# Half-width units for the sixteen least used experts of a mixture-of-experts stage

## The chip, the cores and the metric

The kernel runs as one program on one core of a Trainium2 chip. The metric is the device time of one execution in microseconds (us). The kernel before took 2224.62 us (median of three runs, 2224.14 to 2226.86).

## The reference, cut to what matters

The reference runs a two-layer network of attention mixers and dense feed-forward blocks over 256 tokens of 1024 features, then a block whose last part is a mixture of 32 experts. Only that last part is touched:

```
logits = jnp.dot(xf, w_router) + b_router
vals, idx = lax.top_k(logits, TOP_K)
gate = jax.nn.softmax(vals, axis=-1)
...
up = jnp.dot(xb, w_up[eb]) + b_up[eb]
glu, lin = jnp.split(up, 2, axis=-1)
glu = jnp.minimum(glu, SWIGLU_LIMIT)
lin = jnp.clip(lin, -SWIGLU_LIMIT, SWIGLU_LIMIT)
act = glu * jax.nn.sigmoid(SWIGLU_ALPHA * glu) * (lin + 1.0)
return jnp.dot(act, w_down[eb]) + b_down[eb]
```

Every token goes to 4 of 32 experts (`TOP_K` is 4), so 1024 token-expert pairs are spread over the 32 experts. Each expert has an up matrix of 1024 x 2048 and a down matrix of 1024 x 1024 in float32: 12 MiB, all of which is read once. With the reference's inputs the pairs fall unevenly. The three experts that the kernel takes first whatever their use (0, 11 and 22) have 5, 44 and 43 pairs. The other 29, from the most to the least used, have 99, 86, 78, 63, then 59, 49, 47, 47, 46, 30, 29, 27, and then 25, 25, 23 and so on down to 3.

## The kernel before, in words

Everything before the experts is as it was, but for one small table of constants and the order of a few instructions around it. The experts' stage starts near 1228 us of the span and lasts to its end.

An expert's weights come from main memory as 12 chunks of 128 x 2048 float32 (1 MiB each): chunks 0 to 3 for the gate half of the up product, 4 to 7 for the linear half, 8 to 11 for the down product. They land in a ring of 22 buffers (`RING`). SyncE's queue issues the loads in the order of first use (lines 1945 and 1948), and each waits until the chunk that had its buffer has been used for the last time. For the first 22 loads the buffer is memory that the mixer before used, so these wait for the mixer's last readers and writers there. A semaphore lane is used by every eighth load, so at most eight are under way.

The work is done in units of 64 slots (`CAP`). The tokens of a unit are gathered by a product with a one-hot matrix (`pick`, `gather`, lines 1730 to 1755), two units at a time. Then `products` (line 1778) multiplies: the 64 gathered tokens are the stationary operand of 128 rows x 64 columns, and a chunk streams past in two halves of 512 columns, the first half into PSUM partitions 0 to 63, the second into 64 to 127, so that the 1024 output columns stand as two column blocks one above the other. `expert_gate` and `expert_act` do the activation on VectorE and ScalarE, `expert_turn` transposes, `expert_down` multiplies again, and `expert_out` (line 1837) adds the result to the four accumulators of the output, by a scatter matrix `sp` that `spread` (lines 1757 to 1773) makes. The result is split into a rounded part `yh` and a rest `yl`.

Four of the experts (the four most used besides the three that are fixed) get two units each; all others get one. That makes 36 units. The down product of a unit is done between the two up products of the next. A pair of units has one gather, in four pieces between the products.

If any expert has more pairs than its units have slots, a flag is set and `overflow` runs further passes over all experts at the end.

Of the kernel before, what the change touches and what calls it, by code (L numbers as in the profile page):

```python
# [19 lines left out]
P = 128  # L20
# [136 lines left out]
DOUBLE = (15, 9, 23, 5)  # L157
STEPS = list(range(len(FIXED))) + list(DOUBLE)
STEPS += [s for s in range(NE) if s not in STEPS]
# [3 lines left out]
NU = len(UNITS)  # L163


def _consts3():
    p = np.arange(P)
    slots = np.broadcast_to(TAKEN + np.arange(4 * CAP, dtype=np.float32), (P, 4 * CAP))
# [7 lines left out]
    single = np.broadcast_to(np.array([s not in DOUBLE for s in range(NE)], np.float32), (P, NE))  # L176
    return np.ascontiguousarray(np.concatenate([slots, iota, sel, stri, rank, block, (p % NE).astype(np.float32)[:, None], key,
                                                single], 1))
# [3 lines left out]
M_IOTA = M_SLOTS + 4 * CAP  # L182
# [6 lines left out]
M_SINGLE = M_KEY + NE  # L189
# [132 lines left out]
class Kernel:  # L322
# [1248 lines left out]
    def moe_consts(self, pool):  # L1571

        nc, v, ins = self.nc, self.nc.vector, self.ins
        self.slots = pool.tile([P, 4 * CAP], F32, name="slots")
# [6 lines left out]
        self.single = pool.tile([P, NE], F32, name="single")  # L1581
# [6 lines left out]
        for dst, src in ((self.wr, ins["w_router"]), (self.brc, ins["b_router"].partition_broadcast(P)),  # L1588
                         (self.slots, ins["consts3"][:, M_SLOTS:M_SLOTS + 4 * CAP]),
# [5 lines left out]
                         (self.single, ins["consts3"][:, M_SINGLE:M_SINGLE + NE]), (self.btab, self.btab_dram)):  # L1595
# [27 lines left out]
    def moe_head(self, mp, first_group):  # L1623
# [8 lines left out]
        self.over = mp.tile([1, 3], I32, name="over")  # L1632
        self.order = mp.tile([1, NE], I32, name="order")
        with ExitStack() as ctx:
# [60 lines left out]
            cnt = tp.tile([1, NE + 3], F32, name="cnt")  # L1695
            v.scalar_tensor_tensor(cnt[:, 3:], qs[0:1, NE:2 * NE], float(CAP), self.single[0:1], ALU.is_gt, ALU.mult)
            v.tensor_reduce(cnt[:, 1:2], cnt[:, 3:], AX.X, ALU.max)
            v.tensor_reduce(cnt[:, 2:3], qs[0:1, NE:2 * NE], AX.X, ALU.max)
            v.tensor_scalar(cnt[:, 2:3], cnt[:, 2:3], 2.0 * CAP, None, ALU.is_gt)
            v.tensor_reduce(cnt[:, 0:1], cnt[:, 1:3], AX.X, ALU.max)  # L1700
            v.tensor_copy(self.over, cnt[:, 0:3])
# [28 lines left out]
    def pick(self, of):  # L1730

        v = self.nc.vector
        pr = self.gp.tile([P, 2, len(of) * CAP], F32, tag="pr", name="pr", bufs=2)
        for t in range(2):
            for i, (pos, r) in enumerate(of):
                v.tensor_scalar(pr[:, t, i * CAP:(i + 1) * CAP], self.slots[:, r * CAP:(r + 1) * CAP], pos[:, t:t + 1],
                                self.r2[t], ALU.is_equal, ALU.mult)
        return pr

    def gather(self, xs, j, pr, ps):  # L1740
# [16 lines left out]
    def spread(self, pos, r, gate, pool, bufs):  # L1757

        nc, v = self.nc, self.nc.vector
        pf = self.gp.tile([P, 2, 2, CAP], F32, tag="pf", name="pf")  # L1760
        slots = self.slots[:, r * CAP:(r + 1) * CAP].unsqueeze(1).to_broadcast([P, 2, CAP])
        ps = self.pv()
        for t in range(2):
            v.tensor_scalar(pf[:, t], slots, pos[:, t:t + 1], None, ALU.is_equal)
            nc.tensor.transpose(ps[:, t * P:(t + 1) * P], pf[:, t].rearrange("p a b -> p (a b)"), self.ident)
        for t in range(2):
            nc.tensor.matmul(ps[:, S:S + 1], pf[:, t].rearrange("p a b -> p (a b)"), gate[:, t:t + 1], start=t == 0,  # L1767
                             stop=t == 1, skip_group_check=True)
        sp = pool.tile([P, S], F32R, tag="sp", name="sp", bufs=bufs)
# [12 lines left out]
    def expert_up(self, part, xg, sel, chunk, between={}):  # L1782

        ps = self.sc()
# [4 lines left out]
        self.last_up = self.products(ps, sel, self.btab[:, part], False, True).ins  # L1789
        return ps  # L1790

    def expert_gate(self, ps, pool, gl, sg):
        v = self.nc.vector
        gl = pool.tile([P, 512], F32, tag=gl, name="gl")
        sg = pool.tile([P, 512], F32, tag=sg, name="sg")
# [5 lines left out]
    def expert_act(self, ps, gl, pool, ln="aT"):  # L1801
        v = self.nc.vector
        ln = pool.tile([P, 512], F32, tag=ln, name="ln")
# [4 lines left out]
    def expert_turn(self, a, pool):  # L1808

        pt = self.pt()  # L1810
        for c in range(4):
            self.nc.tensor.transpose(pt[:, c * P:(c + 1) * P], a[:, c * P:(c + 1) * P], self.ident)  # L1812
        aT = pool.tile([P, 512], F32, tag="aT", name="aT")
        self.nc.scalar.copy(aT, pt)
        return quads(aT)

    def expert_down(self, aT, sel, gs, chunk, pool, yh, yl):
        nc, v = self.nc, self.nc.vector
        ps = self.sc()
        self.products(ps, sel, self.btab[:, 2], True, False)  # L1820
        for c in range(4):
            for h in range(2):
                self.products(ps, aT[:, c, 64 * h:64 * h + 64], chunk(8 + c)[:, h * D:h * D + D],
# [427 lines left out]
```

## Time and profile before

| | |
|---|---|
| median of three runs | 2224.62 us |
| profiled execution | 2222.24 us |
| its span in the profile | 2220.5 us |
| TensorE busy | 2184.6 us (98%) |
| VectorE, ScalarE busy | 1152.8 us (52%), 772.7 us (35%) |
| loads of expert chunks | 384 MiB, in 383 loads of 1 MiB and two of 512 KiB |
| granted TensorE clock, mean | 0.996 of full |

The profile shows one execution. In the page's view of 40 equal slices, a digit is the busy share in tenths; PEclk is the clock that TensorE was granted, in tenths of full speed; DMA is the mean busy share of the 16 DMA engines and GB/s what they moved. A float32 product appears as two records of MATMUL, so "x8" of such a group are four products. PEld is TensorE's load of the stationary operand. "SPq" is SyncE's queue, which issues the loads. The text after "<-" in square brackets names what an engine had waited for.

### The profile page before, as it was taken

Reading aid. Unit: us, or ns where it says so; the run is one execution under the profiler, and the core shown is the slowest. Engines: PE = TensorE matmul, PEld = TensorE weight load, DVE = VectorE, ACT = ScalarE, POOL = GpSimd, SP = SyncE. Lnnn points to the kernel's source line nnn. Section 1 sums busy time; section 2 is a strip of 40 time slices with the busy share of each in tenths; the row PEclk is TensorE's granted clock in tenths of the full one; section 3 lists DMA queues with packets and bytes.
Section 4 is the critical chain, followed back from the end, with each engine's and each line's share of the span. In section 5 each row is a group of like instructions: output and inputs, shape, how many; then the busy total and the mean of one; then the engine's idle time right before and its main releaser. Section 6 shows DMA issues by size and latency. Waiting matters only on the chain.

```text
span 2220.5 us, 36133 instructions
## 1 busy us (share of the span) xinstructions
PE 2184.6 (98%) x14352; PEld 1516.0 (68%) x14352; DVE 1152.8 (52%) x2537; ACT 772.7 (35%) x1431; POOL 95.2 (4%) x147
## 2 busy tenths in 40 slices
PE   8999999999999999999999999999999999999997
PEld 8999889999999989999987433333333333333332
DVE  6777778776889887875886322222222222222122
ACT  5545556454444555544574211111111111111111
POOL 1001001221001001001000000000000000000000
PEclk9999999999999999999999999999999999999998
DMA  6655326776664534765534999998999999999995
GB/s 245 209 183 183 133 105 225 270 270 231 247 245 165 190 105 162 256 246 172 186 143 200 420 421 397 374 421 341 379 421 374 387 421 421 421 384 421 421 421 205
DMA packets 93536, 634.10 MB, mean 286 GB/s; under 512 B 12960, under 2 KB 14112, under 8 KB 18224
## 3 DMA queue, kind: packets, MB, share of 16 engines
q1 hardware_dynamic: 87072, 619.63, 71.5%
q0 software_dynamic: 2288, 7.28, 0.9%
q10 hardware_dynamic: 4000, 4.81, 0.7%
q8 instruction: 115, 1.88, 0.3%
q14 instruction: 61, 0.50, 0.1%
HBM read 626.16 MB, written 5.51 MB: 284 GB/s over the span
## 4 chain that ended last, share of the span: by engine, by line
PE 92%; DVE 5%; DMA 1%; issue 1%; ACT 1%; SPq 0%; ACTq 0%; DVEq 0%
PE sc L1778 35%; PE acc L349 11%; PE acc L351 11%; PE acc L350 11%; PE sc L349 3%; PE sc L350 3%; PE sc L351 3%; PE acc L1837 2%; PE pv L1746 2%; PE pt L1746 2%; PE sc L789 1%; DVE wlo L309 1%; PE pv L867 1%; PE pt L1812 1%; DVE xg L1755 1%; PE pt L854 1%
## 5 line engine op out<-in xcount | busy, mean ns | idle before, releaser
L1778 PE MATMUL sc<-ring,xg 128*64 128x512 f32 x2304 | 554.3, 601 | 0.0
L349 PE MATMUL acc<-xh,whi 128*128 128x256 f32 (+1 forms) x1776 | 507.7, 286 | 7.0 <-ACT whi L308 7.0
L351 PE MATMUL acc<-xh,wlo 128*128 128x256 f32 (+1 forms) x1776 | 505.1, 284 | 1.1 <-DVE wlo L309 1.1
L350 PE MATMUL acc<-xl,whi 128*128 128x256 f32 (+1 forms) x1776 | 501.8, 283 | 1.8 <-DVE xl L399 1.8
L309 DVE TENSOR_TENSOR wlo<-wraw,whi 128x1024 fp32r<-128x1024 f32 (+1 forms) x362 | 440.8, 1220 | 115.7 <-ACT whi L308 112.7
L308 ACT CAST whi<-wraw 128x1024 fp32r<-128x1024 f32 (+1 forms) x362 | 375.5, 1043 | 311.3 <-issue 101.3
L349 PEld LDWEIGHTS acc<-xh,whi 128*128 128x128 f32 x1776 | 338.0, 190 | 9.9 <-ACT whi L308 7.2
L350 PEld LDWEIGHTS acc<-xl,whi 128*128 128x128 f32 x1776 | 338.3, 190 | 2.7 <-DVE xl L399 2.6
L351 PEld LDWEIGHTS acc<-xh,wlo 128*128 128x128 f32 x1776 | 337.9, 190 | 1.6 <-DVE wlo L309 1.6
L1778 PEld LDWEIGHTS sc<-ring,xg 128*64 128x64 f32 x2304 | 146.9, 136 | 241.5 <-issue 226.7
L1778 PE MATMUL sc<-ring,aT 128*64 128x512 f32 x1152 | 253.6, 592 | 0.0
L349 PE MATMUL sc<-hh,whi 128*128 128x256 f32 x704 | 199.7, 284 | 0.0
L350 PE MATMUL sc<-hl,whi 128*128 128x256 f32 x704 | 199.2, 283 | 0.0
L351 PE MATMUL sc<-hh,wlo 128*128 128x256 f32 x704 | 199.2, 283 | 0.0
L1778 PEld LDWEIGHTS sc<-ring,aT 128*64 128x64 f32 x1152 | 82.6, 137 | 149.9 <-issue 141.5
L1755 DVE TENSOR_SCALAR xg<-pv,acol,modc 128x64 f32<-128x64 f32 x140 | 38.4, 336 | 245.2 <-PE pv L1746 245.2
L349 PEld LDWEIGHTS sc<-hh,whi 128*128 128x128 f32 x704 | 135.0, 192 | 2.5 <-issue 2.5
L350 PEld LDWEIGHTS sc<-hl,whi 128*128 128x128 f32 x704 | 135.1, 192 | 0.0
L351 PEld LDWEIGHTS sc<-hh,wlo 128*128 128x128 f32 x704 | 135.1, 192 | 0.0
L1828 DVE SCALAR_TENSOR_TENSOR yl<-sc,gs,yh 128x512 fp32r<-128x512 f32 x36 | 27.0, 751 | 206.5 <-ACT yh L1827 206.5
L1771 ACT CAST sp<-pv 128x256 fp32r<-128x256 f32 x36 | 13.4, 372 | 257.1 <-PE pv L1767 257.1
L1827 ACT ACTIVATE yh<-sc,gs 128x512 fp32r<-128x512 f32 x36 | 24.7, 687 | 212.0 <-PE sc L1778 212.0
(497 smaller groups left out, 2437.5 us busy)
## 6 DMA issues: line engine op xcount, KB each, us to landing
ring<-in_experts_dram SPq DMA_DIRECT2D x383, 1024.0 KB, 19.7
wraw<-in_weights_dram SPq DMA_DIRECT2D x178, 1024.0 KB, 4.9
wraw<-in_w_ada_dram SPq DMA_DIRECT2D x24, 1024.0 KB, 5.0
skew<-g POOLq DMA_DIRECT2D x8, 264.0 KB, 6.1
wraw<-in_weights_dram SPq DMA_DIRECT2D x4, 512.0 KB, 3.5
bias_dram<-b POOLq DMA_DIRECT2D x8, 208.0 KB, 5.3
w<-skew POOLq DMA_DIRECT2D x8, 200.0 KB, 5.8
bias<-bias_dram ACTq DMA_DIRECT2D x1, 1040.0 KB, 10.2
```

Source lines behind the costliest of these rows:

```text
L308: self.nc.scalar.copy(hi[:, a:b], r[:, o + a:o + b])
L309: self.nc.vector.tensor_tensor(lo[:, a:b], r[:, o + a:o + b], hi[:, a:b], ALU.subtract)
L349: nc.tensor.matmul(out, wh, xh, start=first, stop=False, skip_group_check=True)
L350: nc.tensor.matmul(out, wh, xl, start=False, stop=False, skip_group_check=True)
L351: nc.tensor.matmul(out, wl, xh, start=False, stop=last, skip_group_check=True)
L789: nc.tensor.matmul(ps[:, t * S:(t + 1) * S], q[:, t * P:(t + 1) * P], k, start=t == 0, stop=t == 1, skip_group_check=True)
L1746: nc.tensor.matmul(ps[:, i * w:(i + 1) * w], self.x[:, j + i, t * P:(t + 1) * P], pr[:, t], start=t == 0 and i == 0, stop=t == 1, skip_gro ...
L1755: nc.vector.tensor_scalar(x[:, j + i], o, a, b, ALU.mult, ALU.add)
L1778: m = self.nc.tensor.matmul(ps[64 * h:64 * h + 64], lhs, rhs[:, h * 512:h * 512 + 512], start=first, stop=last, skip_group_check=True)
L1827: nc.scalar.activation(yh, ps, AF.Copy, scale=gs)
L1828: v.scalar_tensor_tensor(yl, ps, gs, yh, ALU.mult, ALU.subtract)
L1837: self.nc.tensor.matmul(self.out[t][h], sp[rows, t * P:(t + 1) * P], ys[q][rows], start=False, stop=q == 1, skip_group_check=True)
```

## The change

The experts are sorted into kinds by their place in the order of use (`KINDS`): three fixed ones (F) and nine of middle use (M) with one unit of 64 slots, the four most used (D) with two of 64, and the sixteen least used (L) with one unit of 32 slots. There are 36 units as before. The order in which the experts come is now a pattern of seven, four times over: M L D L M L L.

For an L unit `products` issues four products of 32 columns by 256 in place of two of 64 by 512: the 1024 output columns stand as four column blocks in PSUM partitions 0 to 31, 32 to 63, 64 to 95 and 96 to 127. Everything after it in that unit works on 256 columns instead of 512. `spread` makes two copies of the scatter matrix for an L unit, each with the rows of the other column block set to zero, and `expert_out` issues eight products of 256 columns in place of four of 512 for each half of the tokens, each with 64 rows as before. A gather serves up to 128 slots, so up to four units; there are 15 gathers instead of 18. The evacuation of a gather is one instruction for all its units instead of one for each. The overflow path and the test that leads to it are rewritten for the new number of slots. The table `slots` becomes 128 columns instead of 256, and a table `part` of two columns is added; both lie below the ring in the same stack of memory, so that the ring's buffers move by 504 bytes in each partition.

```diff
 FIXED = (0, 11, 22)
-DOUBLE = (15, 9, 23, 5)
...
+KINDS = "FFFM" + 4 * "MLDLMLL"
+STEPS = [s for kind in "FDML" for s in range(NE) if KINDS[s] == kind]
 RANK = [STEPS.index(s) for s in range(NE)]
-UNITS = [(s, r) for s in range(NE) for r in range(1 + (s in DOUBLE))]
+UNITS = [(s, o, n) for s in range(NE)
+         for o, n in {"D": ((0, CAP), (CAP, CAP)), "L": ((0, CAP // 2),)}.get(KINDS[s], ((0, CAP),))]
...
-        self.slots = pool.tile([P, 4 * CAP], F32, name="slots")
+        self.slots = pool.tile([P, 2 * CAP], F32, name="slots")
...
+        self.part = pool.tile([P, 2], F32, name="part")
...
-    def gather(self, xs, j, pr, ps):
+    def gather(self, x, j, pr, ps):
...
-            for n, x in enumerate(xs):
-                o = ps[:, i * w + n * CAP:i * w + n * CAP + CAP]
-                if j % 4 == 0 or j == 6 and len(xs) == 1:
-                    nc.scalar.activation(x[:, j + i], o, AF.Identity, bias=b, scale=a)
-                else:
-                    nc.vector.tensor_scalar(x[:, j + i], o, a, b, ALU.mult, ALU.add)
...
+            o = ps[:, i * w:(i + 1) * w]
+            if j % 4 == 0:
+                nc.scalar.activation(x[:, j + i], o, AF.Identity, bias=b, scale=a)
+            else:
+                nc.vector.tensor_scalar(x[:, j + i], o, a, b, ALU.mult, ALU.add)
...
-        nc.scalar.copy(sp, ps[:, 0:S])
+        k = CAP // n
+        sp = pool.tile([P, 2, S], F32R, tag="sp", name="sp", bufs=bufs)[:, 0:k]
+        for c in range(k):
+            nc.scalar.activation(sp[:, c], ps[:, 0:S], AF.Copy, scale=1.0 if k == 1 else self.part[:, c:c + 1])
...
     def products(self, ps, lhs, rhs, first, last):
-        for h in range(2):
-            m = self.nc.tensor.matmul(ps[64 * h:64 * h + 64], lhs, rhs[:, h * 512:h * 512 + 512], start=first, stop=last,
+        n = lhs.shape[1]
+        w = D * n // P
+        for h in range(P // n):
+            m = self.nc.tensor.matmul(ps[n * h:n * h + n, 0:w], lhs, rhs[:, h * w:h * w + w], start=first, stop=last,
                                       skip_group_check=True)
...
     def expert_out(self, ys, sp, ts=(0, 1)):
+        w = ys[0].shape[1]
         for t in ts:
             for q in range(2):
-                for h in range(2):
-                    rows = slice(64 * h, 64 * h + 64)
-                    self.nc.tensor.matmul(self.out[t][h], sp[rows, t * P:(t + 1) * P], ys[q][rows], start=False, stop=q == 1,
-                                          skip_group_check=True)
+                for c in range(sp.shape[1]):
+                    for h in range(2):
+                        rows = slice(CAP * h, CAP * h + CAP)
+                        self.nc.tensor.matmul(self.out[t][h][:, c * w:c * w + w], sp[rows, c, t * P:(t + 1) * P], ys[q][rows],
+                                              start=False, stop=q == 1, skip_group_check=True)
```

Two places show how instructions moved. The first is TensorE's order in one unit, from the down product of the unit before on: `aT` is the transposed activation, `xg` the gathered tokens, `yh` and `yl` the two parts of a result, and the last figure is partitions x columns of the output. Before, for a unit of 64 slots after a unit of 64:

```order
L1778 MATMUL sc<-ring,aT 64x512 x16
L1778 MATMUL sc<-ring,xg 64x512 x6
L1837 MATMUL acc<-yh,sp 128x512 x2
L1837 MATMUL acc<-yl,sp 128x512 x2
L1778 MATMUL sc<-ring,xg 64x512 x4
```

And now, for an L unit after an L unit:

```order
L1794 MATMUL sc<-ring,aT 32x256 x32
L1794 MATMUL sc<-ring,xg 32x256 x12
L1858 MATMUL acc<-yh,sp 128x256 x4
L1858 MATMUL acc<-yl,sp 128x256 x4
L1794 MATMUL sc<-ring,xg 32x256 x8
```

The products of such a unit are twice as many, each of half the columns out of half the stationary operand; their places in the unit are the same.

The second place is SyncE's queue at the first loads into the ring, with the semaphores that each waits for: PE, DVE and Pool count the instructions of TensorE, VectorE and GpSimd, DMAHW and DMASW with a number are the lanes of loads. Before:

```order
L1948 DMA ring<-in_experts_dram 128x2048 [waits PE_49,Pool_49]
L1948 DMA ring<-in_experts_dram 128x2048
L1948 DMA ring<-in_experts_dram 128x2048 [waits DMAHW4_49,DVE_49]
L1948 DMA ring<-in_experts_dram 128x2048 [waits DMASW4_49,DMASW3_49,DMASW6_49,DMASW2_49,DMASW0_49]
L1948 DMA ring<-in_experts_dram 128x2048 [waits DMAHW1_49,PE_49]
L1948 DMA ring<-in_experts_dram 128x2048 [waits DMAHW3_49,DMAHW2_49]
L1948 DMA ring<-in_experts_dram 128x2048 x2
```

And now:

```order
L1973 DMA ring<-in_experts_dram 128x2048 [waits PE_49,Pool_49]
L1973 DMA ring<-in_experts_dram 128x2048 x2
L1973 DMA ring<-in_experts_dram 128x2048 [waits DMASW4_49,DMASW3_49,DMASW6_49,DMASW2_49,DMASW0_49]
L1973 DMA ring<-in_experts_dram 128x2048 [waits DMAHW2_49]
L1973 DMA ring<-in_experts_dram 128x2048 [waits DMAHW3_49,DVE_49]
L1973 DMA ring<-in_experts_dram 128x2048 [waits DMAHW5_49,DMAHW4_49,DVE_49]
L1973 DMA ring<-in_experts_dram 128x2048
```

Before, the third load waits for VectorE: by the count it waits for, for the mixer's last weight split (line 309), which VectorE began at 1192.11 us in that trace. Now the seventh load waits for that count, and the sixth for that of an earlier weight split, the one that VectorE began at 1159.98 us in the trace of the kernel before. The counts that the new first load waits for are of transposes at line 1429 of the kernel before, which ran before 1098 us. The waits for DMASW lanes are for transfers of GpSimd's queue that are long past in both.

## Rows read from the trace of the kernel before

**Rows 1.** The page: the span, and the part in 40 equal slices of 55.5 us each.

```profile
span 2220.5 us, 36133 instructions
...
PE   8999999999999999999999999999999999999997
...
PEclk9999999999999999999999999999999999999998
DMA  6655326776664534765534999998999999999995
GB/s 245 209 183 183 133 105 225 270 270 231 247 245 165 190 105 162 256 246 172 186 143 200 420 421 397 374 421 341 379 421 374 387 421 421 421 384 421 421 421 205
```

**Rows 2.** Busy time of the engines in stretches: the stretch, its length, then busy us and instructions of PE, PEld, DVE, ACT and POOL, the granted clock, the DMA engines' busy share and GB/s.

```profile
1161.00:1194.00 33.00, 32.67 (x195) 23.08 (x194) 25.26 (x134) 20.65 (x67) 0.00 (x0) 1.00 0.00 1
1230.00:1370.00 140.00, 139.45 (x704) 54.23 (x704) 33.29 (x92) 18.39 (x42) 0.00 (x0) 1.00 1.01 421
1370.00:1400.00 30.00, 29.72 (x150) 11.23 (x148) 6.31 (x17) 3.56 (x8) 0.00 (x0) 1.00 0.87 348
1550.00:1580.00 30.00, 30.00 (x150) 10.84 (x146) 4.24 (x9) 4.15 (x9) 0.00 (x0) 1.00 0.80 323
1194.00:2190.00 996.00, 990.99 (x5016) 392.39 (x5018) 229.59 (x639) 139.97 (x321) 0.00 (x0) 1.00 0.98 403
```

**Rows 3.** The waits, of TensorE from 1194 to 2206 us and of SyncE's queue from 1150 us on: who waited for whom, us in total, times, the longest.

```profile
PE pv L1765 <- DVE xg L1755: 4.7, 17, 0.3
...
SPq L1945 <- PE sc L1778: 244.0, 108, 22.1
...
SPq L1948 <- DVE md L1328: 39.2, 1, 39.2
```

**Rows 4.** The chain of work that ended last, two of its pieces: start us, us, what. They are the same place in a pair of units, sixteen pairs apart.

```profile
1281.30 13.46 PE sc L1778 x64
...
2149.21 13.46 PE sc L1778 x64
```

**Rows 5.** The timeline of TensorE within one pair of units: start us, us, engine, line, operation, output and operands, shapes, records.

```profile
1339.39 7.04 PE L1778 MATMUL sc<-ring,aT 128*64 128x512 f32 x32
1346.26 2.75 PE L1778 MATMUL sc<-ring,xg 128*64 128x512 f32 x12
...
1375.05 1.16 PE L1746 MATMUL pt<-pr,x 128*128 128x128 f32 x8
1376.14 1.08 PE L1778 MATMUL sc<-ring,xg 128*64 128x512 f32 x4
1377.15 0.50 PE L1837 MATMUL acc<-yh,sp 64*128 64x512 f32 x2
```

**Rows 6.** The timeline around line 507, much earlier in the kernel, the one place where four products of 32 columns stand side by side: TensorE, and its loads of the stationary operand.

```profile
480.73 1.06 PE L507 MATMUL pt<-mod,ones 128*32 128x512 f32 x8
481.72 0.38 PE L349 MATMUL sc<-hh,whi 128*128 128x256 f32 x1
...
480.73 0.16 PEld L507 LDWEIGHTS pt<-mod,ones 128*32 128x32 f32 x8
```

**Rows 7.** The loads of expert chunks: the timeline of SyncE's queue at the first of them, the page's row of their issues (KB each and median us from issue to landing), and two weight splits in the timeline of VectorE.

```profile
1151.03 0.86 SPq L1948 DMA_DIRECT2D ring<-in_experts_dram  x2
1193.35 59.23 SPq L1948 DMA_DIRECT2D ring<-in_experts_dram  x30
...
ring<-in_experts_dram SPq DMA_DIRECT2D x383, 1024.0 KB, 19.7
...
1159.98 1.23 DVE L309 TENSOR_TENSOR wlo<-wraw,whi 128x1024 fp32r<-128x1024 f32 x1 [1.65 <-ACT whi L308]
...
1192.11 1.21 DVE L309 TENSOR_TENSOR wlo<-wraw,whi 128x1024 fp32r<-128x1024 f32 x1
```

**Rows 8.** Busy time in stretches of 2 us, where the stream of chunks sets in and where it ends; columns as in rows 2.

```profile
1194.00:1196.00 2.00, 2.00 (x12) 0.92 (x12) 1.75 (x6) 0.76 (x2) 0.00 (x0) 1.00 0.83 201
...
2188.00:2190.00 2.00, 2.00 (x12) 0.98 (x14) 0.00 (x0) 0.00 (x0) 0.00 (x0) 1.00 0.71 287
```

**Rows 9.** Busy time at the start of the kernel, the one stretch in which TensorE waits often; columns as in rows 2.

```profile
5.00:10.00 5.00, 3.73 (x16) 3.30 (x16) 4.08 (x8) 4.92 (x13) 1.61 (x2) 1.00 1.01 371
10.00:15.00 5.00, 2.87 (x14) 2.46 (x15) 2.70 (x5) 3.48 (x8) 3.91 (x4) 0.79 1.00 423
15.00:20.00 5.00, 5.00 (x26) 5.00 (x26) 2.81 (x4) 3.92 (x5) 0.00 (x0) 0.53 0.99 374
20.00:25.00 5.00, 5.00 (x44) 5.00 (x43) 4.79 (x13) 1.46 (x2) 0.00 (x0) 1.00 0.60 197
```

**Rows 10.** The timeline of all engines at the end: the last down product, the two parts of its result, and the last product into the accumulators.

```profile
2196.18 7.09 PE L1778 MATMUL sc<-ring,aT 128*64 128x512 f32 x32
...
2203.31 0.69 ACT L1827 ACTIVATE yh<-sc,gs 128x512 fp32r<-128x512 f32 x1 [8.16 <-PE sc L1778]
...
2204.03 0.75 DVE L1828 SCALAR_TENSOR_TENSOR yl<-sc,gs,yh 128x512 fp32r<-128x512 f32 x1 [8.58 <-ACT yh L1827]
...
2204.84 0.73 PE L1837 MATMUL acc<-yl,sp 64*128 64x512 f32 x4
```

More of the change, by code (lines that the diff above doesn't have):

```diff
@@ L175, in _consts3 @@
     block = (p[:, None] // NE == p[None, :] // NE).astype(np.float32)
-    single = np.broadcast_to(np.array([s not in DOUBLE for s in range(NE)], np.float32), (P, NE))
+    room = np.broadcast_to(np.array([sum(n for x, _, n in UNITS if x == s) for s in range(NE)], np.float32), (P, NE))
+    part = np.stack([p // 32 % 2 == c for c in range(2)], 1).astype(np.float32)
     return np.ascontiguousarray(np.concatenate([slots, iota, sel, stri, rank, block, (p % NE).astype(np.float32)[:, None], key,
-                                                single], 1))
+                                                room, part], 1))
 M_SLOTS = 0
-M_IOTA = M_SLOTS + 4 * CAP
+M_IOTA = M_SLOTS + 2 * CAP
 M_SEL = M_IOTA + NE
@@ L188 @@
 M_KEY = M_COL + 1
-M_SINGLE = M_KEY + NE
+M_ROOM = M_KEY + NE
+M_PART = M_ROOM + NE
 def _expert_chunks(up, down):
@@ L1788, in expert_up @@
                 f()
-        self.last_up = self.products(ps, sel, self.btab[:, part], False, True).ins
+        self.last_up = self.products(ps, sel[:, 0:n], self.btab[:, part], False, True).ins
         return ps
@@ L1808, in expert_turn @@
     def expert_turn(self, a, pool):
+        w = a.shape[1]
         pt = self.pt()
-        for c in range(4):
+        for c in range(w // P):
             self.nc.tensor.transpose(pt[:, c * P:(c + 1) * P], a[:, c * P:(c + 1) * P], self.ident)
         aT = pool.tile([P, 512], F32, tag="aT", name="aT")
-        self.nc.scalar.copy(aT, pt)
-        return quads(aT)
+        self.nc.scalar.copy(aT[:, 0:w], pt[:, 0:w])
+        n = w // P
+        m = P * w // D
+        return [aT[:, k % n * P + k // n * m:k % n * P + k // n * m + m] for k in range(KD)]
     def expert_down(self, aT, sel, gs, chunk, pool, yh, yl):
         nc, v = self.nc, self.nc.vector
-        ps = self.sc()
-        self.products(ps, sel, self.btab[:, 2], True, False)
+        n = aT[0].shape[1]
+        w = D * n // P
+        ps = self.sc()[:, 0:w]
+        self.products(ps, sel[:, 0:n], self.btab[:, 2], True, False)
         for c in range(4):
             for h in range(2):
-                self.products(ps, aT[:, c, 64 * h:64 * h + 64], chunk(8 + c)[:, h * D:h * D + D],
-                              False, c == 3 and h == 1)
-        yh = pool.tile([P, 512], F32R, tag=yh, name="yh")
-        yl = pool.tile([P, 512], F32R, tag=yl, name="yl")
+                self.products(ps, aT[4 * h + c], chunk(8 + c)[:, h * D:h * D + D], False, c == 3 and h == 1)
+        yh, yl = [pool.tile([P, 512], F32R, tag=t, name=t)[:, 0:w] for t in (yh, yl)]
         nc.scalar.activation(yh, ps, AF.Copy, scale=gs)
@@ L1886, in more_slots @@
                 sel = self.select(bsel, ep)
-                for r in rs:
+                for r in range(2):
                     raw = {}
@@ L1963, in moe, with group @@
         groups, spreads = {}, {}
-        def group(u, pos):
-            of = UNITS[u:u + 2]
-            pr = self.pick([(pos(e), r) for e, r in of])
-            xs = [gp.tile([P, KD, CAP], F32, tag="xg", name="xg", bufs=3) for _ in of]
-            groups.update({u + i: x for i, x in enumerate(xs)})
-            return [lambda j=j, ps=(self.pt, self.pv)[j // 2 % 2]: self.gather(xs, j, pr, ps()) for j in range(0, KD, 2)]
+        def group(first, pos):
+            of = UNITS[slice(*first)]
+            pr = self.pick([(pos(e), o, n) for e, o, n in of])
+            x = gp.tile([P, KD, P], F32, tag="xg", name="xg", bufs=2)[:, :, 0:pr.shape[2]]
+            at = 0
+            for i, (_, _, n) in enumerate(of):
+                groups[first[0] + i] = x[:, :, at:at + n]
+                at += n
+            return [lambda j=j, ps=(self.pt, self.pv)[j // 2 % 2]: self.gather(x, j, pr, ps()) for j in range(0, KD, 2)]
         def first_group():
-            for f, ps in zip(group(0, lambda e: self.pos[:, :, FIXED[e]]), (self.sc, self.sc, self.pt, self.pv)):
+            for f, ps in zip(group(GROUPS[0], lambda e: self.pos[:, :, FIXED[e]]), (self.sc, self.sc, self.pt, self.pv)):
                 f(ps=ps)
@@ L2011, in down @@
                 return self.expert_down(o["a"], o["sel"], o["gs"], o["chunk"], ep, "yh", "yl")
+        starts = {first: (first, end) for first, end in GROUPS}
         old = None
-        for u, (e, r) in enumerate(UNITS):
+        for u, (e, _, _) in enumerate(UNITS):
             n = {}
@@ L2023, in moe @@
             steps = post() if last else [lambda: slots(u + 1)]
-            if u % 2 and not last:
-                steps = group(u + 1, lambda e: self.spos[:, :, e]) + steps
+            if u + 1 in starts:
+                steps = group(starts[u + 1], lambda e: self.spos[:, :, e]) + steps
             if u:
```

102 lines of the change are left out of this document (55 added, 47 removed).

## The prediction

> **What bounds the kernel now.** I read the 40 slices of the page first [rows 1]. The reader should see two halves: up to slice 21 the DMA engines are busy half of the time, and from slice 23 on they stand at 9 with 421 GB/s, with single slices at 341 to 397. TensorE is at 9 everywhere and its clock full. So in the experts' stage two resources are near their end at once, and the question is which of them waits for the other.
>
> Next the waits [rows 3]. TensorE waits for nothing but 4.7 us of gather evacuations; it never waits for a chunk. SyncE's queue waits 244 us for TensorE's products, up to 22.1 us at a time: it has a chunk to load and no free buffer. So TensorE sets the pace and the transfers follow. The stretches [rows 2] show how close it is: 1.01 busy share and 421 GB/s from 1230 to 1370 us, but 0.87 from 1370 to 1400 and 0.80 from 1550 to 1580.
>
> The slack of the transfers is counted so. A chunk is 1,048,576 bytes, at 421 GB/s 2.49 us; that fits the 19.7 us from issue to landing with eight under way [rows 7]. Two chunks are loaded early, at 1151 us, the other 382 in one stream that sets in at 1194.4 us (0.83 of 2 us at once) and ends at 2189.4 us (0.71 of 2 us) [rows 7, 8]. 382 x 2.49 = 951 us, so without a stop it would end at 2145.6 us: 43.8 us of the stream are stops. The mean of 403 GB/s over 996 us [rows 2] says the same, 4.3% or 43 us.
>
> TensorE's pace: the same place in a pair of units comes 16 pairs later at 2149.21 instead of 1281.30 us [rows 4], 54.24 us for a pair and 27.12 for a unit; 36 units take 976 us. An expert's 12 chunks take 29.9 us, 32 experts 956. A single unit is faster than its transfer, a double one (54.2) far slower; together TensorE is slower by 20 us.
>
> **The change part by part.** *Products of the L units.* Sixteen products of a down part take 6.87 us (1339.39 to 1346.26) [rows 5], 0.86 us for a pair of column blocks; the three parts of a unit 20.6 us, and 6.5 us are gather, transposes, scatter and the rest. For an L unit the same weights stream as four blocks of 256 columns. From below that is half, 0.43 us for the four, if four blocks run side by side as two do; from above 0.86 us, if they run two by two. The nearest rows: four products of 32 columns by 512 take 1.06 us with the next instruction 0.99 us after their start [rows 6]; two of 64 by 512 take 1.08 and 1.01 us (1376.14 to 1377.15) [rows 5]. Four blocks cost what two cost, so I take half. Their eight loads of the stationary operand took 0.16 us [rows 6], less than 0.43. An L unit is then 27.12 - 10.3 = 16.8 us, 16 of them save 165 us. The activation, the transposes and the two parts of the result on half the columns only get shorter, off the path except at the end. Three gathers fewer save 3 x 4 pieces x 1.1 us (1375.05 to 1376.14) [rows 5] = 13 us. The second copy of the scatter matrix is one more ScalarE instruction per L unit; ScalarE is busy 140 of 996 us [rows 2], which hides it. TensorE's demand falls from 976 to 20 x 27.12 + 16 x 16.8 - 13 = 798 us.
>
> *The first loads.* The ring lies 504 bytes elsewhere, and so the queue's wait of 39.2 us [rows 3] stands before the seventh load, no longer before the third. Loads three to five can go at 1151 us, the sixth when the weight split begun at 1159.98 us is done; the seventh goes at 1193.35 us, as the third did [rows 7]. From 1161 to 1194 us the DMA engines are idle, 0.00 and 1 GB/s [rows 2], so four chunks land in time that nothing uses: 378 instead of 382 are left. That is 4 x 2.49 = 10 us, which counts only if the transfers set the end. The bounds are 0 us, if one of the other waits is late, and 10; I take 10.
>
> *What is late next.* With 798 us of work against 941 us of transfers TensorE waits and the chunks set the pace: the gain on TensorE beyond the stops of the stream is lost. The stream ends at 1194.4 + 378 x 2.49 = 2135.6 us plus what stops remain. A stop needs a full ring. TensorE's first product is near 1228 us in both, when some 20 chunks have landed; it gains on the transfers by 2.8 us with each full unit and 13.1 us with each L unit, and gives back 24 us at a double expert, four times. One pattern of seven (two M, four L, one D) takes TensorE 175.7 us and the transfers 209, so after the first pattern TensorE is always close behind the stream. Only the first double expert finds a well filled ring. From below the stops are 0, from above the 43.8 us of now; the nearest is one stop like that of 1370 to 1400 us, 0.13 x 30 = 4 us [rows 2]. I take 4: the stream ends at 2139.6 us.
>
> *The end.* Now the last product ends at 2203.3 and the span at 2220.5 us, 17.2 us later [rows 1, 10]. The last half chunk is used some 2 us after it lands (a landing like the ones above, then two rounds of products). The two parts of the result, 0.69 and 0.75 us [rows 10], halve: -0.7 us. Against that, I add 0.7 us for a clock that may stand low there (below). 2139.6 + 2 + 17.2 = 2158.8 us.
>
> *Sum.* Span 2158.8 against 2220.5, -61.7 us. The profiled execution was 1.7 us above its span (2222.24), so 2160.5; the median of the runs is 2.4 us above the profiled execution, so 2163 us for the median.
>
> **The clock.** TensorE will be idle for 15% of the stage, in L stretches for 44%. At the kernel's start there is such a stretch [rows 9]: with 2.87 of 5 us busy, waiting for operands, the granted clock fell to 0.79 and then to 0.53, close to the lower level of 1.2 GHz, and after 5 us of full work it was 1.00 again. So I expect dips in the L stretches. At the lower level an L unit takes 33.6 us, more than its 29.9 us of chunks; TensorE falls behind, is then busy without a gap, and gets the clock back, as the last of these rows shows. The lag is a few us, and the ring takes it.
>
> The Trainium skill, in "TensorE: Matmul & The Clock Gate", section "HAM oscillation — how this bites in real kernels", says that a kernel whose work on each loaded slice is shorter than the wait for the next starts every slice at the low clock. By that rule every chunk of an L unit would be worked at 1.2 GHz; it is the rival below, and the first three of rows 9 agree with the fall.
>
> The skill's "DMA: Bandwidth & Descriptors", section "Where 436 GB/s comes from", has main memory bind one core at about 358 GB/s. By that 378 chunks would take 1107 us and the stream would end at 2302 us. The trace disagrees: 421 GB/s for 140 us [rows 2].
>
> **The rivals.**
> *Low clock all along (slower).* If the clock stayed low through all L units, they would take 16 x 33.6 = 538 us, with the others 1080 us against 976: 2222 + 104 = 2326 us. It decides from the point where an L unit costs what a unit costs now, 27.1 us, 1.6 times its time at full clock; up to 24.9 us ((941 - 542) / 16) the transfers still hide it. For it speaks the fall in rows 9; against it the recovery there, since a unit too slow for its chunks leaves no gaps.
> *Column blocks two by two.* Then an L unit keeps its 20.6 us of products, and only the gathers' 13 us and some shorter steps go: 2224 - 17 = 2207 us. Against it speaks line 507 [rows 6].
> *Stops remain.* The double experts keep filling the ring, or slow L units pile up before them, and half of the 43.8 us stays: 2163 + 18 = 2181 us. For it: the stops of now [rows 2]; against it: the balance of a pattern, 176 against 209 us.
> *The overflow pass runs.* It would load every expert again, at least 956 us more. With the reference's inputs the sixteen least used hold at most 25 pairs for 32 slots, the next nine 59 for 64, the doubles 99 for 128, so I give it nothing.
>
> **How the numbers follow.** The transfers set the pace: 0.78, with 2154 to 2175 us as its own range (no stop at one end, no early loads at the other). Stops remain: 0.10. Two by two: 0.05. Low clock all along: 0.04. Something else of no effect: 0.03. The range of 2152 to 2188 us holds the first and most of the second case. About 0.2% is what a measurement of this kernel can tell from none. Faster by more: 0.78 + 0.10 + 0.05, so 0.93; within: 0.03; slower: 0.04.
>
> **What would show it.** In the profile after: 421 GB/s in every slice from 1230 us to the stream's end near 2139 us; SyncE's waits for products down from 244 to under 40 us; TensorE waiting 50 to 130 us for chunks, busy share near 85%; PEclk below 9 in some of the later slices; six loads issued before 1162 us; four products of 256 columns in 0.43 us at full clock. Wrong would be a stream that still stops for over 20 us, or TensorE with no waits at all.

## The result and the profile after

The changed kernel takes 2166.2 us (median of four runs, 2163.59 to 2168.76), the kernel before beside it 2224.69 us: a ratio of 0.9735, 95% interval 0.9718 to 0.9752. The forecast was 2163 us. The profiled execution took 2168.29 us, with a span of 2166.4 us.

The page of the changed kernel, with its engine totals, its slices and its chain of waits:

```profile
PE 2053.7 (95%) x15984; PEld 1493.2 (69%) x15984; DVE 1114.5 (51%) x2452; ACT 747.0 (34%) x1363; POOL 93.9 (4%) x147
...
PE   8999999999999999999999999999889788978995
...
PEclk9999999999999999999999999999999999999997
DMA  6555425876765522765534999999999999999996
GB/s 251 209 181 182 143 100 199 306 260 214 254 237 188 209 107 98 266 243 198 204 113 190 382 422 421 420 401 420 421 421 421 421 421 421 421 420 421 421 421 265
...
PE 72%; DMA 22%; DVE 4%; ACT 1%; issue 1%; ACTq 0%; SPq 0%; DVEq 0%
```

Against [rows 1] the slices of 341 to 397 GB/s are gone; one of 401 is left (slice 27), besides slice 23 (382), in which the stream sets in. TensorE's digits now fall to 7 and 8 in the last third, and a fifth of the chain that ended last is loads of chunks. TensorE's waits from 1194 to 2160 us, which answer to [rows 3] (engine and line, for whom: us in total, times, longest):

```profile
PE sc L1794 <- DMA ring<-in_experts_dram: 80.4, 102, 2.9
PE pv L1777 <- DVE xg L1767: 1.8, 7, 0.3
```

It waited for no chunk before and now does so 102 times. The roles have changed. SyncE's queue from 1150 to 2170 us:

```profile
SPq L1970 <- DMA ring<-in_experts_dram: 538.4, 287, 3.5
SPq L1970 <- PE sc L1794: 124.0, 82, 11.4
SPq L1973 <- DVE md L1337: 31.8, 1, 31.8
...
SPq L1973 <- PE sc L1794: 23.9, 13, 3.4
```

The queue's waits for products are 124.0 + 23.9 = 148 us, far over the 40 us that I had named. (Before they were 254 us: the 244.0 of [rows 3] and 9.6 more at line 1948.) Whether these waits stop the stream is read from stretches (length, PE, PEld, DVE, ACT, POOL busy, granted clock, DMA share, GB/s):

```profile
1196.00:1198.00 2.00, 2.00 (x12) 0.95 (x9) 1.08 (x3) 0.09 (x2) 0.00 (x0) 1.00 0.84 332
1224.00:1434.00 210.00, 209.62 (x1272) 86.53 (x1274) 51.39 (x156) 28.65 (x61) 0.00 (x0) 1.00 1.01 420
1434.00:1464.00 30.00, 30.00 (x258) 11.68 (x252) 5.22 (x13) 2.96 (x6) 0.00 (x0) 1.00 0.94 385
1464.00:2138.00 674.00, 593.67 (x4916) 248.15 (x4912) 116.30 (x313) 73.84 (x159) 0.00 (x0) 0.95 1.01 421
2138.00:2140.00 2.00, 1.18 (x20) 0.54 (x20) 0.00 (x0) 0.36 (x1) 0.00 (x0) 1.00 0.83 338
2140.00:2142.00 2.00, 1.83 (x16) 1.73 (x16) 0.48 (x1) 0.38 (x2) 0.00 (x0) 0.65 0.62 254
2144.00:2146.00 2.00, 1.35 (x24) 0.42 (x16) 0.00 (x0) 0.00 (x0) 0.00 (x0) 1.00 0.53 219
2148.00:2150.00 2.00, 2.00 (x26) 0.72 (x21) 0.00 (x0) 0.00 (x0) 0.00 (x0) 0.50 0.05 18
```

They hardly do: 674 us without a gap, and one stop at the first double expert, 30 x (421 - 385) / 421 = 2.6 us. But the stream doesn't end at full rate, as it did before [rows 8]: it tapers for 10 us from 2138 us on. The early loads, and the products of L units, are read from the timelines of SyncE and of TensorE:

```profile
1152.29 10.53 SPq L1973 DMA_DIRECT2D ring<-in_experts_dram  x6
```

```profile
2115.22 1.91 PE L1794 MATMUL sc<-ring,xg 128*32 128x256 f32 x32
2117.06 0.44 PE L1829 MATMUL pt<-ident,gl 128*128 128x128 f32 x2
...
2147.43 3.58 PE L1794 MATMUL sc<-ring,aT 128*32 128x256 f32 x32 [1.39 <-DMA ring<-in_experts_dram]
```

Six loads are issued before 1163 us instead of two [rows 7]. Sixteen products (32 records) take 1.84 us to the next instruction, a transpose: at most 0.46 us for the four column blocks (a longer row of them, further down, gives 0.435). The last sixteen take 3.58 us, at a granted clock of 0.50, the lower of its two levels.

**Where the 54.1 us of span went.** Before, the stream set in at 1194.4 us, ran for 951 us and stopped for 43.8 us in all; the last down product ended 13.9 us behind it, and 17.2 us of tail followed. After, it sets in at 1195.8 us (+1.4: in this execution the first load of the ring goes 1.3 us later, at 1152.29 against 1151.03 us), moves four chunks fewer (-10.0) and stops for 2.6 us (-41.2). The last down product ends at 2151.0 us, 11.4 us after the 2139.6 us that these terms give (-2.5), and the tail is 15.4 us (-1.8).

### The profile page after: what moved, and what is told of

It reads as the page before. It is cut to its first block, busy times and chain, and to the rows that moved or that the text cites. A ratio compares the mean times of both kernels' runs of the same rounds, so it can differ in the third digit from the quotient of the medians.

```text
span 2166.4 us, 39235 instructions
## 1 busy us (share of the span) xinstructions
PE 2053.7 (95%) x15984; PEld 1493.2 (69%) x15984; DVE 1114.5 (51%) x2452; ACT 747.0 (34%) x1363; POOL 93.9 (4%) x147
## 4 chain that ended last, share of the span: by engine, by line
PE 72%; DMA 22%; DVE 4%; ACT 1%; issue 1%; ACTq 0%; SPq 0%; DVEq 0%
DMA ring<-in_experts_dram 21%; PE sc L1794 17%; PE acc L358 12%; PE acc L360 11%; PE acc L359 11%; PE sc L358 3%; PE sc L360 3%; PE sc L359 3%; PE sc L798 1%; PE acc L1858 1%; DVE wlo L318 1%; PE pv L876 1%; PE pv L1759 1%; PE pt L1759 1%; PE pt L863 1%
## 5 line engine op out<-in xcount | busy, mean ns | idle before, releaser
L1794 PE MATMUL sc<-ring,xg 128*32 128x256 f32 (+1 forms) x3328 | 465.5, 482 | 31.9 <-DMA ring<-in_experts_dram 31.8
L1794 PEld LDWEIGHTS sc<-ring,xg 128*32 128x32 f32 (+1 forms) x3328 | 137.6, 122 | 242.9 <-issue 147.3
L1794 PE MATMUL sc<-ring,aT 128*32 128x256 f32 (+1 forms) x1664 | 218.8, 496 | 48.6 <-DMA ring<-in_experts_dram 48.6
L1794 PEld LDWEIGHTS sc<-ring,aT 128*32 128x32 f32 (+1 forms) x1664 | 76.0, 126 | 171.1 <-issue 83.3
L1847 DVE SCALAR_TENSOR_TENSOR yl<-sc,gs,yh 128x512 fp32r<-128x512 f32 (+1 forms) x36 | 22.8, 632 | 232.7 <-ACT yh L1846 232.7
L1767 DVE TENSOR_SCALAR xg<-pv,acol,modc 128x128 f32<-128x128 f32 (+2 forms) x58 | 20.6, 397 | 169.1 <-PE pv L1759 169.1
L1846 ACT ACTIVATE yh<-sc,gs 128x512 fp32r<-128x512 f32 (+1 forms) x36 | 21.3, 592 | 237.4 <-PE sc L1794 237.4
L1776 DVE TENSOR_SCALAR pf<-slots,both 128x128 f32<-128x128 f32 x72 | 17.5, 283 | 163.6 <-PE pv L1779 163.6
## 6 DMA issues: line engine op xcount, KB each, us to landing
ring<-in_experts_dram SPq DMA_DIRECT2D x383, 1024.0 KB, 19.8
```

The lines of the kernel that those rows point to most:

```text
L1794: m = self.nc.tensor.matmul(ps[n * h:n * h + n, 0:w], lhs, rhs[:, h * w:h * w + w], start=first, stop=last, skip_group_check=True)
L1847: v.scalar_tensor_tensor(yl, ps, gs, yh, ALU.mult, ALU.subtract)
```

## The experiments

The theory: the transfers set the end once TensorE's work in the stage is below them, and what TensorE saves beyond that is lost. Each time stands with its ratio to the kernel before on the same chip, and the ratio's 95% interval; the changed kernel's ratios are 0.9735 and, in a second series, 0.9733.

**Is it the transfers?** Here sixteen chunks are left out ("..." marks what is left out of a diff):

```diff
+        held = lambda e, c: (e, 10 if c == 11 and KINDS[e] == "L" else c)
+        seq = list(dict.fromkeys(held(*n) for n in uses))
...
+                c = held(e, c)[1]
```

> The changed kernel with the last chunk of each of the 16 least used experts not loaded (the chunk before it is used in its place, so the output is another): 368 chunks instead of 384, the work of TensorE unchanged. If the transfers set the end: 16 x 2.49 = 40 us less, 2126 us (2122 to 2132). If TensorE sets it: no change.

2129.32 us, 0.957 (0.9555 to 0.9585); the changed kernel beside it, which follows further down, took 2165.65. So it is 36.3 us less, of the 39.8 us of sixteen chunks. Most of the rest lies in the first stop:

```profile
1425.00:1455.00 30.00, 30.00 (x252) 12.44 (x248) 6.83 (x20) 3.29 (x7) 0.00 (x0) 1.00 0.89 350
```

Here that stop is 30 x (421 - 350) / 421 = 5.1 us, 2.5 us longer, as one would expect when fewer chunks are needed and the ring is full sooner. 39.8 - 2.5 = 37.3 us. The transfers set the end.

**What does TensorE need?** Here a quarter of the chunks is left out, so that TensorE binds:

```diff
+        held = lambda e, c: (e, c - (c % 4 == 3))
...
+                c = held(e, c)[1]
```

> The changed kernel with three of the twelve chunks of every expert not loaded (the chunk before is used in their place, so the output is another): 288 chunks, 717 us of transfers, the work of TensorE unchanged. The transfers no longer bind, and the time measures what TensorE itself needs for the units. Theory: the run without narrow units (2217 us, TensorE bound) less 16 narrow units and 3 gathers; with the estimate of 10.3 us a unit 2217 - 165 - 13 = 2039 us, with the 0.46 us of four products seen in the trace (9.6 us a unit) 2050 us; 2030 to 2060. Rival: column blocks two by two and no faster units, 2200 us.

2039.98 us, 0.9159 (0.9145 to 0.9173). No wait for a chunk is left. The stretch from the first product of the units to the last, and 24 products in a row with the instruction behind them:

```profile
1233.00:2026.00 793.00, 789.87 (x6500) 343.12 (x6499) 167.78 (x452) 103.56 (x221) 0.00 (x0) 1.00 0.89 356
...
2016.92 2.80 PE L1794 MATMUL sc<-ring,aT 128*32 128x256 f32 x48
2019.53 0.29 PE L1794 MATMUL sc<-btab,bsl 96*32 96x256 bf16 x4
```

The units take from 1232.93 to 2025.45 us, 792.5 us; I had worked out 798. The mean granted clock is 1.00. The 24 products (48 records) take 2.61 us to the next instruction, 0.435 us for each four column blocks. So the forecast of 2039 us, by 10.3 us a unit, came true, and not that of 2050 us, by the 0.46 us.

**Does every narrow unit count?** First none of the 16 is narrow, then half of them are:

```diff
-KINDS = "FFFM" + 4 * "MLDLMLL"
+KINDS = "FFFM" + 4 * "MMDMMMM"
```

> The changed kernel with all 16 narrow units made full ones (pattern M M D M M M M): what is left of the change is the order of the experts and the six early loads. TensorE's demand is 976 us again, over the transfers. Theory: 2222 us (2218 to 2228), the stream stops for some 50 us, TensorE waits for no chunk. Rival: order and early loads carry a part of the gain, under 2210 us.

2216.91 us, 0.9956 (0.9942 to 0.997). It is TensorE bound as expected, but 8.5 us faster than the kernel before, where I expected 2 or 3: 1 us below the stated range. From the first to the last product it takes 969.3 us (1230.76 to 2200.10), so 16 narrow units and three gathers (13 us) are worth 969.3 - 792.5 = 176.8 us, 10.2 us a unit.

```diff
-KINDS = "FFFM" + 4 * "MLDLMLL"
+KINDS = "FFFM" + 4 * "MLDMMLM"
```

> The changed kernel with 8 of the 16 narrow units made full ones again (the pattern of seven is M L D M M L M, 18 gathers instead of 15). TensorE's demand rises by 8 x 10.3 + 13 = 95 us, from 798 to 893 us, still under the 941 us of the transfers. Theory: the time stays at 2166 us, 2162 to 2173 (a fuller ring at the double experts may stop the stream some more). Rival, by which each narrow unit is worth its own TensorE time: a good half of the gain goes, 2195 us or more.

2173.74 us, 0.9766 (0.9753 to 0.978): 7.5 us more than with all 16, just outside the range and far from the rival's 29. TensorE still waits for chunks, 24.5 us in all. The waits, a stretch and the timeline show where the time goes, at two places:

```profile
PE sc L1794 <- DMA ring<-in_experts_dram: 24.5, 31, 1.6
...
1436.00:1466.00 30.00, 30.00 (x152) 11.39 (x152) 4.91 (x11) 3.62 (x7) 0.00 (x0) 1.00 0.84 336
```

```profile
2151.58 7.09 PE L1794 MATMUL sc<-ring,aT 128*64 128x512 f32 x32
```

The stop at the first double expert is 6.1 instead of 2.6 us. And the last unit is a full one: its down product runs 7.09 us at a stretch, when the last bytes have landed (the DMA share is 0.04 from 2152 us on). So eight narrow units lift the bound, and what the other eight add is read at these two places.

**The early loads.** First the changed kernel with the ring back at its old place, then the kernel before with the ring at the new one:

```diff
-        self.slots = pool.tile([P, 2 * CAP], F32, name="slots")
+        self.slots = pool.tile([P, 2 * CAP + 126], F32, name="slots")[:, 0:2 * CAP]
```

> The changed kernel with its ring of chunk buffers 504 bytes further along, where it lay before. The wait for the last weight split then stands before the third load again: two early loads instead of six. If the transfers set the end (the theory), four chunks of 2.49 us more go through the stream: 2166 + 10 = 2176 us, and the stream sets in as before and ends 10 us later. If TensorE sets the end, or the early chunks only fill the ring sooner, the time stays at 2166 us (within 3).

2174.38 us, 0.9765 (0.9751 to 0.9778): 6.7 us more by the ratios, 8.2 by the medians. The stop at 1435 us is not there:

```profile
1436.00:1466.00 30.00, 30.00 (x266) 11.80 (x260) 5.21 (x13) 2.96 (x6) 0.00 (x0) 1.00 1.01 420
```

Four chunks fewer are loaded ahead, so the ring isn't full there: 10 - 2.6 = 7.4 us.

```diff
-        self.slots = pool.tile([P, 4 * CAP], F32, name="slots")
+        self.slots = pool.tile([P, 2 * CAP + 2], F32, name="slots")
...
```

> The kernel before with nothing changed but the ring's place (504 bytes less ahead of it; the passes for overflow, which these inputs don't reach, read the first slot numbers again). Six early loads instead of two. Theory: TensorE sets the pace in the kernel before, so the four chunks become 10 us more of stops and the time stays at 2224.7 us (2221 to 2227). Rival: the early loads are worth their 10 us by themselves, 2215 us.

2223.19 us, 0.9992 (0.9983 to 1.0001): this can't be told from no change. The same four chunks are worth nothing where TensorE binds.

**The 8.5 us without narrow units.** TensorE's waits in the last run, then in the one without narrow units:

```profile
PE pv L1765 <- DVE xg L1755: 4.7, 17, 0.3
PE acc L1837 <- ACT yh L1827: 1.4, 2, 0.8
```

```profile
PE acc L1858 <- ACT yh L1846: 1.4, 2, 0.8
```

The 17 waits for evacuations of gathers [rows 3] are gone. The change evacuates a piece in one instruction for all its units. That part alone, on top of the early loads:

```diff
-            for n, x in enumerate(xs):
-                o = ps[:, i * w + n * CAP:i * w + n * CAP + CAP]
-                if j % 4 == 0 or j == 6 and len(xs) == 1:
+            o = ps[:, i * w:(i + 1) * w]
+            if j % 4 == 0:
...
```

> The kernel before with the six early loads (2223.2 us, TensorE bound) and with one part of the change more: each piece of a gather is evacuated in one instruction for both units, no longer in one for each. Theory: the 17 waits of TensorE for these evacuations (4.7 us) go, and with them the 8.5 us by which the run without narrow units was faster than before: 2218 us (2216 to 2220). Rival: the order of the double experts did that, 2223 us.

2218.8 us, 0.9965 (0.9951 to 0.9978). Its interval overlaps with that of the run without narrow units (0.9956) and not with that of the early loads alone. So the evacuations account for most of it, 0.9992 - 0.9965 or 6.0 us; the 2.0 us that are left (0.9965 - 0.9956) are within the noise, and whether the order of the experts has a part in them is not shown.

**The taper at the end.** The trace records sixteen landings for every load. Those of the stream's first load lie within 0.5 us, but already from the second on they are 1.3 to 2.0 us apart, and near its end 9.4 to 11 us. From the stop at 1435 us on the spread grows in steps of 1.3 to 1.6 us (at 1462, 1585, 1726, 1882, 2020 and 2153 us by these records' clock, which is 10.5 us ahead of the span's). Each step comes 3 to 4 us behind every eighth packet of TensorE's instructions: the 13th, the 21st and so on to the 53rd, the last in the stream. In the kernel before there were 40, and the stops of the stream let the late engines catch up: the spread fell from 3.9 to 1.7 us at one. To test it, the same columns were issued in twice as many products:

```diff
-        for h in range(P // n):
...
+        for g in range(0, w, w // 2):
+            for h in range(P // n):
...
```

> The changed kernel with every product of the experts issued as two of half the columns: the same columns and bytes, 5304 more products and as many more loads of the stationary operand, 10,608 instructions. Theory: TensorE's instructions are fetched in packets of 16 KB by the same DMA engines, 53 packets in the stage now, some 41 more; 8 packets hold the slowest DMA engine up by 1.5 us (its landings fell 9.4 us behind the earliest ones with 53 packets), so the taper at the end grows from 9 to 17 us and the time by 5 to 8 us. Rival 1: the taper has another cause, no change (within 2 us). Rival 2: half as wide products cost TensorE so much more that it sets the pace again: over 20 us more, no waits for chunks.

(The output of this variant is another. Its instructions, columns and bytes are those described, but the "5304 more products" are records of MATMUL, two for a float32 product.) 2175.14 us, 0.9775 (0.9761 to 0.9788), 9.5 us more than the changed kernel beside it, where 5 to 8 were expected. Queues from 1194 to 2152 us (packets, MB, share of 16 engines), of the changed kernel run again and of this one:

```profile
q8 instruction: 54, 0.88, 0.4%
```

```profile
q8 instruction: 94, 1.54, 0.7%
```

And the end of this one, with TensorE's waits for chunks:

```profile
2142.00:2144.00 2.00, 0.69 (x28) 0.41 (x16) 0.00 (x0) 0.00 (x0) 0.00 (x0) 1.00 0.69 281
2154.00:2156.00 2.00, 2.00 (x50) 1.54 (x44) 0.00 (x0) 0.00 (x0) 0.00 (x0) 0.62 0.40 164
...
PE sc L1795 <- DMA ring<-in_experts_dram: 78.3, 101, 2.4
```

There are forty packets more; the spread of the last landings is 15.0 us instead of 9.7, and the taper 15 us instead of 10. TensorE still waits 78 us for chunks, so the second rival falls. Of the 10.1 us between the two spans, 3.1 lie before the first load of the ring (1153.66 against 1150.52 us), where the two profiled executions of the changed kernel differ too, by 1.8 us; 7.0 us lie behind it. The theory holds in count and direction.

The run with eight narrow units, which was made for another end, fits it. The sixteen parts of the stream's last load, and the packets of the stream up to there:

| run | packets | spread |
|---|---|---|
| eight narrow units | 47 | 8.1 us |
| changed kernel, two profiles | 53 | 10.9 and 9.7 us |
| every product in two halves | 95 | 15.0 us |

The bytes are the same in all of them, so it isn't the bytes that set the spread. Whether the packets alone delay those engines was not tried apart from the instructions that they carry.

**The same kernel again, and three attempts at more.**

> The changed kernel once more, unchanged, on the chip of the three runs beside it: 2166 us (2163 to 2170), and again a stream that runs at 421 GB/s to some 10 us before its end and then tapers.

2165.65 us, 0.9733 (0.972 to 0.9746). It tapers as before. Its last sixteen products (32 records):

```profile
2144.84 1.07 PE L1794 MATMUL sc<-ring,aT 128*32 128x256 f32 x16 [1.39 <-DMA ring<-in_experts_dram]
2146.09 0.64 PE L1794 MATMUL sc<-ring,aT 128*32 128x256 f32 x8 [0.18 <-DMA ring<-in_experts_dram]
2147.34 0.64 PE L1794 MATMUL sc<-ring,aT 128*32 128x256 f32 x8 [0.61 <-DMA ring<-in_experts_dram]
```

They run at a clock of 1.00, so the low clock at the end is not in every execution. They take from 2144.84 to 2147.98 us, 3.14 us, since they wait for the two halves of the last chunk. At the low clock the same sixteen took 3.58 us, so it cost 0.4 us there and not the half of 3.58.

```diff
-SLOTS = (2, 3, 13, 0, 1, 16, 15, 17, 4, ...
+SLOTS = (2, 3, 13, 0, 1, 16, 17, 15, 4, ...
```

> The changed kernel with two entries of the ring's order exchanged, so that the seventh load goes into a buffer that waits for the weight split before the last one (at 1182 us in the trace) and not for the last (1193 us). One chunk more lands before the stream sets in. If the transfers set the end: 2.5 us less than the changed kernel beside it. If they don't: no change.

2165.75 us, 0.9734 (0.9721 to 0.9748): this gained nothing, though the load went 11 us earlier. The same stretch of the run above and of this one:

```profile
1230.00:1235.00 5.00, 5.00 (x24) 1.75 (x25) 2.01 (x8) 0.27 (x1) 0.00 (x0) 1.00 1.01 419
```

```profile
1230.00:1235.00 5.00, 5.00 (x25) 1.76 (x21) 1.91 (x8) 0.27 (x1) 0.00 (x0) 1.00 0.77 293
```

In these 5 us (421 - 293) / 421 x 5 = 1.5 us are lost; at the first double expert it is 0.4 us more (382 instead of 388 GB/s from 1425 to 1455 us), which leaves 0.6 of the 2.5 us, less than the runs can tell. The likely reading is that the ring is full at 1230 us, before the first products (from 1228 us) have freed a buffer: with six early loads the 22 buffers are used up.

```diff
-KINDS = "FFFM" + 4 * "MLDLMLL"
+KINDS = "FFFM" + "LMLDMLL" + 3 * "MLDLMLL"
```

> The changed kernel with the first pattern of seven in another order (L M L D M L L instead of M L D L M L L): two narrow units stand ahead of the first double expert, so the ring has more free buffers when TensorE stays 54 us with that expert. If the stop of the stream near 1435 us is paid in full at the end: 2.6 us less than the changed kernel, 2163 us. If not: 2166 us.

2164.32 us, 0.9719 (0.9706 to 0.9732). The stop is gone:

```profile
1435.00:1440.00 5.00, 5.00 (x28) 2.04 (x24) 0.75 (x1) 1.49 (x3) 0.00 (x0) 1.00 1.02 423
```

But the sixteen parts of its last load land 12.3 us apart, where it was 9.7 and 10.9 us: without a stop the late engines don't catch up, and a part of the 2.6 us may go there.

> Both at once: the seventh early load, which alone came back as a stop at 1230 us and a longer one at 1435 us, and the first pattern in the order L M L D M L L. If the ring is full at 1230 us already before the first product frees a buffer, the seventh early load is worth nothing there either, 2163 us as with the order alone; if its gain was lost at the double expert alone, 2160.5 us.

2163.49 us, 0.9718 (0.9705 to 0.9731): the same as the order alone, again with a gap at 1230 us (0.81). This is the fastest version, some 3 us under the changed kernel by the ratios, as the theory of the stop has it; but the intervals overlap, so that gain isn't settled.

## Why the prediction was right, and where it was off

- *TensorE sets the pace before, the transfers after.* This was right, and is shown from both sides: four chunks are worth nothing before and some 7 us after; 16 chunks fewer are worth 36.3 us.
- *TensorE's demand, 798 us.* It is 792.5 us. A narrow unit saves 10.2 us (10.3 predicted), and four products take 0.435 us (0.43): 24 x (0.86 - 0.435) = 10.2 us, so the saving is that of the products, as said. The prediction passed over one part of the change, the evacuation of a gather in one piece. In the kernel before that part is worth 6.0 us by the ratios, about the whole difference.
- *The early loads, -10 us.* The six loads went as said and the four chunks were saved; the first stop takes 2.6 us of it back. I had counted a stop there apart, at 4 us.
- *Stops of the stream, 4 us at the first double expert.* There were 2.6 us, at the place named.
- *"SyncE's waits for products down from 244 to under 40 us".* This was wrong: it is 148 us, and was 254 before. The step took a wait of the queue for a stop of the stream. A load is issued some 20 us before it lands (median 19.8 us), so eight are under way, and the queue can wait while the DMA engines go on. From 1224 to 1434 us it waited 113 of these 148 us, up to 11.4 us at a time, and the stream ran at 420 GB/s. In the kernel before, too, 254 us of such waits stood against 43.8 us of stops.
- *The end of the stream, 2139.6 us, and 2 us to the last product.* This is the term that was mis-sized. Two errors of 1.4 us (set-in and stops) cancel, and the last product ended 9.4 us later than said. The sum let all DMA engines finish together. By the landing records (on the span's clock) the first of the last load's sixteen parts lands at 2139.0 us, about where the sum had the whole stream end, and the last at 2149.9 us; the last product ends 1.1 us behind it. In the kernel before the last load's parts lay 2.2 us apart, so nothing there showed it. A chunk is there when the last of its sixteen parts is. The Trainium skill, "DMA: Bandwidth & Descriptors", section "Why a DMA increments its semaphore by 16 and not by 1", says that the engines of one transfer finish independently and only the sixteenth report means that all has landed. The trace agrees, with sixteen landings per load, up to 11 us apart.
- *The tail, 17.2 us.* It is 15.4 us. In the run without narrow units it is 15.9 us, so most of the 1.8 us is not the narrow units' doing; what it is stays open.
- *The clock.* There are dips in the L stretches, as said: the mean granted clock is 0.83 to 0.89 in three of the five stretches of 30 us below, and 1.00 in the first of them and in the second, in which TensorE is busy all the time. They are too short for the sign that I named: in the page's 40 slices PEclk stays at 9 up to the last one (7).

```profile
1494.00:1524.00 30.00, 23.42 (x276) 10.18 (x278) 4.46 (x12) 2.65 (x6) 0.00 (x0) 1.00 1.01 421
1614.00:1644.00 30.00, 30.00 (x216) 12.10 (x216) 6.00 (x17) 4.02 (x8) 0.00 (x0) 1.00 1.01 421
1704.00:1734.00 30.00, 23.11 (x194) 8.73 (x194) 3.45 (x9) 1.86 (x4) 0.00 (x0) 0.83 1.01 420
1914.00:1944.00 30.00, 22.19 (x206) 8.05 (x194) 3.45 (x9) 1.86 (x4) 0.00 (x0) 0.89 1.01 422
2004.00:2034.00 30.00, 25.13 (x140) 10.06 (x142) 3.17 (x8) 2.25 (x5) 0.00 (x0) 0.83 1.01 421
```

  The stream runs at 420 to 422 GB/s through all of them, so the dips cost nothing there. At the end of the profiled execution one cost 0.4 us (0.7 predicted). The prediction read the Trainium skill ("TensorE: Matmul & The Clock Gate", section "HAM oscillation — how this bites in real kernels") as saying that every chunk of an L unit would be worked at the low clock. That isn't what these rows show: TensorE is idle for a fifth of the first stretch, at 1.00. The section tells it of a wait that is long enough for the clock to fall; the waits for chunks here were 0.8 us in the mean (80.4 us in 102 waits) and 2.9 us at the longest.
- *From span to median.* I added 2.4 us, as in the kernel before; here the profiled execution lay 2.1 us above the median. So the span was forecast 7.6 us too low and the median only 3.2: that the median came so close is luck.
- *TensorE's waits before.* The prediction had "nothing but" the 4.7 us of evacuations; there were 1.4 us for two results besides, at the last units, which changes nothing in the sum.

## What to carry to other kernels

When an engine has been the bound, count the next resource's whole time from its first use to its last before valuing the gain: here the 43.8 us of stops, the 10 us of the early loads and the lag at the end were all that could be had from an engine that got 177 us lighter. Gains that come as "earlier" or "fuller" end where the buffers are full; look for the stop that takes them back. A queue's waits are not its stream's stops: read the DMA share of the stretch.

## What the runs showed of the hardware that was not expected

- The 16 DMA engines drift apart in a stream that hardly pauses: the sixteen parts of one load land 1.3 to 2.0 us apart at its start, and 9.7 to 10.9 us apart at its end, some 950 us later.
- The drift goes with the number of instructions: 47 packets of 16 KB of TensorE's instructions in the stream and 8 us of spread, 53 packets and 10 to 11 us, 95 packets and 15 us. Four column blocks instead of two double the products of a unit, which is a price of narrow products that TensorE's own time doesn't show.
